# A hybrid decoder layer on one core: early weights loaded in 4 KB rows for two column groups in turn, and index queries computed for tokens 64 to 255 alone

## The chip, the cores and the metric

One core of a Trainium2 chip runs the kernel. The metric is device microseconds (us) of one execution, less is better. TensorE (PE) multiplies, VectorE (DVE), ScalarE (ACT) and GpSimd (POOL) prepare and collect, SyncE (SP) issues the loads, all from one queue in the order of the program. PEld is TensorE's load of the stationary operand.

## What is computed

256 tokens, width 4096, float32 in and out. The part that matters here:

```python
mod = jax.nn.silu(c) @ w_ada + b_ada               # 4096 x 12288
shift, scale, gate = jnp.split(mod, 3, axis=-1)
h = rms_norm(x, norm_g) * (1 + scale) + shift
z = h @ w_in                                       # 4096 x 15520
uA, vA, gA, qB, kB, vB, gB, qI, kI, wI = split(z)  # qI: 32 heads x 128 index queries
dots  = einsum('bqhd,bsd->bqhs', qI, kI)
score = einsum('bqh,bqhs->bqs', wI, relu(dots))    # causal; the best 64 keys of each query are kept
...                                                # attention, spatial gating, norms
x + gate * (concat([yA, yB]) @ w_out)
```

A query keeps min(256, 256/4) = 64 keys. Tokens 0 to 63 have at most 64 causal keys, so for them all causal keys are kept whatever the scores are.

## The kernel before

A float32 product is made of three fast ones. A weight tile `raw` is split into `whi` (ACT, L408: a rounded copy) and `wlo = raw - whi` (POOL and DVE, L414 and L416); h is kept as `hh` and `hl` in the same way. Then hh x whi, hl x whi and hh x wlo are summed in PSUM (`multiply`, L419).

The work is a list of steps, `stream`. One step takes 2 of the 32 chunks of 128 rows of a weight and up to 512 columns (one column group) and has 12 matmuls: 2 chunks x 3 products x 2 halves of 128 tokens. `step(t)` (L441) records, in this order, the load of the weights of step t + 3 (`load_w`, 4 buffers `raw`), the split of step t, the collecting of a group that ended two steps earlier (`add_to`, L793: PSUM is added to the group's sum in SBUF by two DVE additions), some of the side work, and the matmuls of step t.

The first 368 steps are the early stage, 8 blocks of 46 steps. A block has 4 chunks of h. It goes through 23 column groups of `w_in`: two of 336 columns (the last part of the index queries, the index key and the head weights, `kw`), and 21 of 512 (index queries `qi`, `v`, `u`, `q`, `k`, `vb`), 2 steps each. h of a block needs its columns of `w_ada`: while block b runs, the DVE op of L196 (called the ada op here) multiplies and adds 32 tiles `wa` for block b + 1, paced evenly by `pace` (L979), about 0.7 in a step. After each ada op the next `wa` is issued into its buffer (2 buffers). `pace(t)` stands before `step(t)`, so in SP's queue a `wa`, which waits for the ada op of that step, stands ahead of the `raw` of that step. On DVE the subtraction is given 320 of the 1024 columns of a step, POOL the other 704.

In block 7 no `wa` is left for h. There the indexer (L490) runs beside the steps: it turns the index queries of each head, multiplies them with the index keys, and adds up the scores. After the early stage come 8 gate groups of 16 steps and 8 output groups of 16 steps, with the attention beside them.

Of the kernel before, what the change touches and what calls it, by code (L numbers as in the profile page):

```python
# [15 lines left out]
P = 128  # L16
# [21 lines left out]
AHEAD = 3  # L38
# [4 lines left out]
def layer(ctx, tc, x, c, w_ada, b_ada, norm_g, w_in, ln_v_g, ln_v_b, w_s, b_s, q_norm_g,  # L43
# [213 lines left out]
    h_hi, h_lo = {}, {}  # L257
# [24 lines left out]

    def keep_h(b, hh, hl):
        for j in range(BLOCKS[b]):
            h_hi[starts[b] + j] = hh[:, j]
            h_lo[starts[b] + j] = hl[:, j]

    def first_h():
# [26 lines left out]
    def make_h(b, accs):  # L315
# [18 lines left out]
        for j in range(0, nk, 2):  # L334
            nc.gpsimd.tensor_sub(hl[:, j], hts[j // 2][:, 0], hh[:, j].bitcast(F32))
            nc.vector.tensor_sub(hl[:, j + 1], hts[j // 2][:, 1], hh[:, j + 1].bitcast(F32))
            if j + 2 == nk:
                keep_h(b, hh, hl)
# [38 lines left out]

    visits = []
    stream = []

    def visit(src, parts, ks, c0, w, read, soon=False, before=None):
        v = dict(src=src, parts=parts, ks=ks, c0=c0, w=w, read=read, soon=soon, before=before)
        visits.append(v)
        for i in range(0, len(ks), 2):
            stream.append((v, i))

    raws = {}
# [13 lines left out]
    def split(t):  # L401

        raw, w = raws.pop(t), stream[t][0]["w"]
        nk = raw.shape[1]
        hi = [sp.tile([P, 512], F32R, name="whi") for _ in range(nk)]
        lo = [sp.tile([P, 512], F32R, name="wlo") for _ in range(nk)]
        for kk in range(nk):
            nc.scalar.activation(hi[kk][:, :w], raw[:, kk, :w], AF.Copy)  # L408
        left = nk * pool_cols[0] * w // 1024 * 2
        for kk in range(nk):  # L410
            cut = w - min(left, w)
            left -= w - cut
            if cut:
                nc.vector.tensor_sub(lo[kk][:, :cut], raw[:, kk, :cut], hi[kk][:, :cut].bitcast(F32))  # L414
            if cut < w:
                nc.gpsimd.tensor_sub(lo[kk][:, cut:w], raw[:, kk, cut:w], hi[kk][:, cut:w].bitcast(F32))  # L416
        halves[t] = hi, lo

    def multiply(t):  # L419

        v, i = stream[t]
# [3 lines left out]
        (ah, al), w, n_k = v["parts"], v["w"], len(v["ks"])  # L425
        nk = len(hi)
        todo = [(part, kk, n) for kk in range(nk) for part in range(2) for n in range(NT)]
        todo += [(2, kk, n) for kk in range(nk) for n in range(NT)]
        if t + 1 == len(stream):
            todo.sort(key=lambda x: x[2])  # L430
        for part, kk, n in todo:
            k = v["ks"][i + kk]
            a = al if part == 1 else ah
            b = lo if part == 2 else hi
            nc.tensor.matmul(v["ps"][n][:, :w], a[k][:, n * P:(n + 1) * P], b[kk][:, :w],  # L435
                             start=(i + kk == 0 and part == 0),
                             stop=(i + kk == n_k - 1 and part == 2))
# [3 lines left out]
    def step(t):  # L441
        load_w(t + AHEAD)
# [10 lines left out]
        v, i = stream[t]  # L453
# [15 lines left out]
    groups["qi7"] = zp.tile([P, NT, 512], F32, name="qi7", tag="qi7")  # L469
    groups["kw"] = zp.tile([P, NT, 160], F32, name="kw", tag="kw")  # L470
    early.append((O_KW - 176, 336, [("qi7", 336, 176), ("kw", 0, 160)]))
    early.append((O_KW - 512, 336, [("qi7", 0, 336)]))
    for g in range(7):
# [16 lines left out]
    def indexer():  # L490
# [24 lines left out]
        wi = small([P, NT, IDX_HEADS], "wi")  # L515
        tp = misc()
# [11 lines left out]
        def turn(g, n):  # L528
            tp = misc()
            for hh in range(4):  # L530
# [546 lines left out]
```

## Time and profile before

| what | us |
|---|---|
| runs (3), median | 1887.4 (1884.28 to 1892.18) |
| the profiled execution's own time | 1888.63 |
| its span, first to last instruction | 1886.9 |
| PE busy | 1824.8 (97%) |
| DVE, POOL, ACT busy | 1447.4 (77%), 1295.3 (69%), 933.8 (49%) |
| bytes moved by DMA | 542.58 MB, 288 GB/s on the mean |

PE busy is the union of matmul records, whose ends are modelled, so it says that PE always had something, not that it ran at its best. A stage is judged by the start times of its matmuls.

### The profile page before, as it was taken

Reading aid. Unit: us, or ns where it says so; the run is one execution under the profiler, and the core shown is the slowest. Engines: PE = TensorE matmul, PEld = TensorE weight load, DVE = VectorE, ACT = ScalarE, POOL = GpSimd, SP = SyncE. Lnnn points to the kernel's source line nnn. Section 1 sums busy time; section 2 is a strip of 40 time slices with the busy share of each in tenths; the row PEclk is TensorE's granted clock in tenths of the full one; section 3 lists DMA queues with packets and bytes.
Section 4 is the critical chain, followed back from the end, with each engine's and each line's share of the span. In section 5 each row is a group of like instructions: output and inputs, shape, how many; then the busy total and the mean of one; then the engine's idle time right before and its main releaser. Section 6 shows DMA issues by size and latency. Waiting matters only on the chain. (4 is left out here: it accounts for less than half of the span.)

```text
span 1886.9 us, 27998 instructions
## 1 busy us (share of the span) xinstructions
PE 1824.8 (97%) x8324; PEld 1490.3 (79%) x8324; DVE 1447.4 (77%) x1762; ACT 933.8 (49%) x1737; POOL 1295.3 (69%) x1339
## 2 busy tenths in 40 slices
PE   5799999999999999999999999999999999999998
PEld 2487878878888888788888777787888888888887
DVE  4666888888888888888777898877777677677754
ACT  4356545344453454444445556566654554444443
POOL 0366777777777777777675546766567777877786
PEclk9899999999999999999999999999999999999999
DMA  9999998999989989999874477876789799899964
GB/s 311 339 338 340 332 322 304 331 316 306 335 304 322 321 300 324 328 309 340 284 207 146 128 224 262 272 257 202 242 281 312 248 323 338 295 307 350 334 212 156
DMA packets 269554, 542.58 MB, mean 288 GB/s; under 512 B 17270, under 2 KB 29784, under 8 KB 269404
## 3 DMA queue, kind: packets, MB, share of 16 engines
q1 hardware_dynamic: 269404, 540.79, 84.6%
q8 instruction: 68, 1.11, 0.2%
q14 instruction: 82, 0.67, 0.1%
HBM read 536.51 MB, written 4.22 MB: 287 GB/s over the span
## 5 line engine op out<-in xcount | busy, mean ns | idle before, releaser
L416 POOL TENSOR_TENSOR wlo<-raw,whi 128x512 fp32r<-128x512 f32 (+1 forms) x1248 | 1220.3, 1004 | 536.9 <-ACT whi L408 448.2
L408 ACT ACTIVATE whi<-raw 128x512 fp32r<-128x512 f32 (+1 forms) x1248 | 730.9, 619 | 834.9 <-DMA raw<-in_w_in_dram 407.5
L414 DVE TENSOR_TENSOR wlo<-raw,whi 128x320 fp32r<-128x320 f32 (+2 forms) x624 | 640.7, 1028 | 323.2 <-ACT whi L408 209.4
L435 PE MATMUL mm_ps<-whi,hh 128*128 128x512 f32 (+1 forms) x1984 | 620.4, 394 | 11.4 <-ACT whi L408 9.4
L435 PE MATMUL mm_ps<-whi,hl 128*128 128x512 f32 (+1 forms) x1984 | 604.9, 386 | 2.4 <-DVE hl L303 2.4
L435 PE MATMUL mm_ps<-wlo,hh 128*128 128x512 f32 (+1 forms) x1984 | 525.4, 386 | 5.7 <-DVE wlo L414 4.1
L196 DVE SCALAR_TENSOR_TENSOR acc<-wa,csil,acc 128x1024 f32<-128x1024 f32 x341 | 436.3, 1279 | 57.1 <-DMA wa<-in_w_ada_dram 56.4
L435 PEld LDWEIGHTS mm_ps<-wlo,hh 128*128 128x128 f32 x1984 | 368.9, 188 | 83.8 <-POOL wlo L416 8.8
L435 PEld LDWEIGHTS mm_ps<-whi,hh 128*128 128x128 f32 x1984 | 363.5, 189 | 90.2 <-ACT whi L408 19.9
L435 PEld LDWEIGHTS mm_ps<-whi,hl 128*128 128x128 f32 x1984 | 371.2, 188 | 77.3 <-DVE hl L303 2.9
L435 PE MATMUL mm_ps<-whi,yh 128*128 128x512 f32 x512 | 158.2, 390 | 0.0
L435 PE MATMUL mm_ps<-whi,yl 128*128 128x512 f32 x512 | 158.0, 389 | 0.0
L435 PE MATMUL mm_ps<-wlo,yh 128*128 128x512 f32 x512 | 137.5, 390 | 0.2
L435 PEld LDWEIGHTS mm_ps<-wlo,yh 128*128 128x128 f32 x512 | 95.9, 188 | 21.2 <-POOL wlo L416 1.5
L435 PEld LDWEIGHTS mm_ps<-whi,yh 128*128 128x128 f32 x512 | 95.9, 188 | 20.4 <-ACT whi L408 0.4
L435 PEld LDWEIGHTS mm_ps<-whi,yl 128*128 128x128 f32 x512 | 96.1, 188 | 20.0
L802 DVE TENSOR_TENSOR qi<-qi,mm_ps 128x512 f32<-128x512 f32 (+2 forms) x126 | 73.2, 616 | 0.0
L217 PE MATMUL acc<-wa,csil 128*1 128x512 f32 x64 | 28.1, 629 | 13.2 <-DMA wa<-in_w_ada_dram 13.2
L802 DVE TENSOR_TENSOR u<-u,mm_ps 128x512 f32<-128x512 f32 x56 | 35.6, 675 | 0.0
L802 DVE TENSOR_TENSOR v<-v,mm_ps 128x512 f32<-128x512 f32 x56 | 35.6, 675 | 0.0
L802 DVE TENSOR_TENSOR q<-q,mm_ps 128x512 f32<-128x512 f32 x56 | 35.6, 675 | 0.0
L222 DVE SCALAR_TENSOR_TENSOR accs<-wa,csil,accs 128x1024 f32<-128x1024 f32 x15 | 19.2, 1283 | 17.9 <-DMA wa<-in_w_ada_dram 17.8
(173 smaller groups left out, 797.2 us busy)
## 6 DMA issues: line engine op xcount, KB each, us to landing
raw<-in_w_in_dram SPq DMA_DIRECT2D x464, 512.0 KB, 5.9
wa<-in_w_ada_dram SPq DMA_DIRECT2D x384, 512.0 KB, 5.1
raw<-in_w_out_dram SPq DMA_DIRECT2D x128, 512.0 KB, 6.0
raw<-in_w_in_dram SPq DMA_DIRECT2D x32, 336.0 KB, 4.8
xs<-in_x_dram SPq DMA_DIRECT2D x8, 512.0 KB, 5.4
xres<-in_x_dram SPq DMA_DIRECT2D x8, 512.0 KB, 6.8
out_dram<-yt SPq DMA_DIRECT2D x16, 256.0 KB, 3.6
wk<-rb_d SPq DMA_DIRECT2D x16, 128.0 KB, 4.7
```

The costliest lines, as they stand in the source:

```text
L196: nc.vector.scalar_tensor_tensor(dst, src, csil[:, k:k + 1], dst, op0=OP.mult, op1=OP.add)
L217: nc.tensor.matmul(acc[g:g + 1, s, :w], csil[:, k:k + 1], wt[:, s], start=i < 4, stop=i >= KC // 2 - 4)
L222: nc.vector.scalar_tensor_tensor(accs, wt, csil[:, k:k + 1], accs, op0=OP.mult, op1=OP.add)
L408: nc.scalar.activation(hi[kk][:, :w], raw[:, kk, :w], AF.Copy)
L414: nc.vector.tensor_sub(lo[kk][:, :cut], raw[:, kk, :cut], hi[kk][:, :cut].bitcast(F32))
L416: nc.gpsimd.tensor_sub(lo[kk][:, cut:w], raw[:, kk, cut:w], hi[kk][:, cut:w].bitcast(F32))
L435: nc.tensor.matmul(v["ps"][n][:, :w], a[k][:, n * P:(n + 1) * P], b[kk][:, :w], start=(i + kk == 0 and part == 0), stop=(i + kk == n_k - 1 ...
L802: nc.vector.tensor_add(z, z, p)
```

## The change

Three things change together.

1. *Loads.* In the early stage `kw` becomes a group of its own, 160 columns, loaded as one tile of 4 chunks. The other 22 groups (8 `qi`, 14 others, all 512 wide) are taken in pairs. A load is one chunk and 1024 neighbouring columns (rows of 4 KB where they were 2 KB; 512 KB a load as before). A pair of groups goes: chunks 0 and 1 for its first group, the same chunks for its second, chunks 2 and 3 for the first, for the second. `load_w` now issues whatever fits into the 4 buffers; a buffer is free once both groups have been split.
2. *Index queries.* For the `qi` groups, `side_by_side` puts tokens 64 to 127 of h's two parts beside each other (`both`: 64 columns of hh, 64 of hl), so that one matmul with `whi` gives both products for them. The two rows of results are added in the indexer by a matmul with `fold` in place of the transposition. Tokens 0 to 63 are not computed, and their mask is set so that all their causal keys are kept.
3. *Order.* The additions of a group that ended come before the split of the step (`soon=b > 0`), and two `yield`s spread the side work of the later stages.

```diff
+    def side_by_side(b, hts):
+        both = s2.tile([P, BLOCKS[b], 2, 64], F32R, name="both", tag="s2")
+        for i, ht in enumerate(hts):
+            j = slice(2 * i, 2 * i + 2)
+            nc.scalar.activation(both[:, j, 0], ht[:, :, 64:P], AF.Copy)
+            nc.vector.tensor_sub(both[:, j, 1], ht[:, :, 64:P], both[:, j, 0].bitcast(F32))
+        for j in range(BLOCKS[b]):
+            h_both[starts[b] + j] = both[:, j].rearrange("p a b -> p (a b)")
...
+    def visit_pair(src, c0, v0, v1):
+        for i in range(0, len(v0["ks"]), 2):
+            m = [new_load(src, [k], c0, 1024) for k in v0["ks"][i:i + 2]]
+            stream.append((v0, i, [(m[0], 0), (m[1], 0)], 0))
+            stream.append((v1, i, [(m[0], 1), (m[1], 1)], 2))
...
-    def load_w(t):
-        if t >= len(stream) or t in raws:
-            return
-        v, i = stream[t]
-        nk, w, c0 = min(2, len(v["ks"]) - i), v["w"], v["c0"]
-        raw = wp.tile([P, 2, 512], F32, name="raw")
-        raw = raw[:, :nk]
-        nc.sync.dma_start(raw[:, :, :w], v["src"][:, v["ks"][i]:v["ks"][i] + nk, c0:c0 + w])
-        raws[t] = raw
+    def load_w():
+        while len(raws) < min(len(loads), split_loads[0] + WBUFS):
+            nk, w, src = loads[len(raws)]
+            raw = wp.tile([P, 1024], F32, name="raw")
+            raw = raw[:, :nk * w].rearrange("p (k w) -> p k w", k=nk)
+            nc.sync.dma_start(raw, src)
...
-        todo = [(part, kk, n) for kk in range(nk) for part in range(2) for n in range(NT)]
-        todo += [(2, kk, n) for kk in range(nk) for n in range(NT)]
+        for k, b in zip(ks, hi):
+            if v["packed"]:
+                todo += [(0, h_both[k], b), (1, half(ah, k, 1), b), (1, half(al, k, 1), b)]
+            else:
+                todo += [(n, half(a, k, n), b) for a in (ah, al) for n in range(NT)]
+        for k, b in zip(ks, lo):
+            todo += [(n, h_both[k] if v["packed"] and n == 0 else half(ah, k, n), b) for n in range(NT)]
...
     def step(t):
-        load_w(t + AHEAD)
+        load_w()
...
     for b, nk in enumerate(BLOCKS):
-        for c0, w, parts in early:
-            visit(w_in_t, (h_hi, h_lo), list(range(starts[b], starts[b] + nk)), c0, w, add_to(parts, b == 0),
-                  soon=0 < b and nk == 2)
+        ks = list(range(starts[b], starts[b] + nk))
+        vs = [new_visit((h_hi, h_lo), ks, w, add_to(parts, b == 0), packed=parts[0][0].startswith("qi"),
+                        soon=b > 0) for c0, w, parts in early]
+        visit(w_in_t, early[0][0], vs[0], per=nk)
+        for e in range(1, len(early), 2):
+            visit_pair(w_in_t, early[e][0], vs[e], vs[e + 1])
```

On SP, in the middle of block 0, the queue of before (a `wa` is a tile of `w_ada`, a `raw` one of `w_in`; what a row waits for stands in brackets):

```order
L178 DMA wa_1128<-in_w_ada_dram 128x2x512 [waits DMAHW6_49,DVE_49]
L396 DMA raw_1130<-in_w_in_dram 128x2x512 [waits DMAHW3_49,Pool_49]
L178 DMA wa_1156<-in_w_ada_dram 128x2x512 [waits DMAHW0_49,DVE_49]
L396 DMA raw_1158<-in_w_in_dram 128x2x512 [waits DMAHW5_49,Pool_49]
L178 DMA wa_1184<-in_w_ada_dram 128x2x512 [waits DMAHW2_49,DVE_49]
L396 DMA raw_1186<-in_w_in_dram 128x2x512 [waits DMAHW7_49,Pool_49]
```

And the same place in the changed kernel:

```order
L177 DMA wa_1181<-in_w_ada_dram 128x2x512 [waits DMAHW3_49,DVE_49]
L177 DMA wa_1209<-in_w_ada_dram 128x2x512 [waits DMAHW4_49,DVE_49]
L424 DMA raw_1211<-in_w_in_dram 128x1024 [waits DMAHW1_49,Pool_49]
L424 DMA raw_1213<-in_w_in_dram 128x1024 [waits DMAHW2_49,Pool_49]
L177 DMA wa_1237<-in_w_ada_dram 128x2x512 [waits DMAHW7_49,DVE_49]
L177 DMA wa_1261<-in_w_ada_dram 128x2x512 [waits DMAHW0_49,DVE_49]
L424 DMA raw_1263<-in_w_in_dram 128x1024 [waits DMAHW5_49,Pool_49]
L424 DMA raw_1265<-in_w_in_dram 128x1024 [waits DMAHW6_49,Pool_49]
```

Where one weight load was issued in each step, two are now issued in every second step, behind the `wa` of that step.

On DVE, in block 1 of the changed kernel, between the subtractions (`wlo`) of one pair of loads (`raw_3091`, first group, then second group) and the one after:

```order
L854 TENSOR_TENSOR qi0_167<-qi0_167,mm_ps_3051 128x512 [waits PE_49]
L854 TENSOR_TENSOR qi0_167<-qi0_167,mm_ps_3052 128x512 [waits PE_49]
L445 TENSOR_TENSOR wlo_3146<-raw_3091,whi_3144 128x320 [waits DMAHW4_49,Activation_49]
L195 SCALAR_TENSOR_TENSOR acc_2721<-wa_3113,csil_160,acc_2721 128x1024 [waits DMAHW5_49,DVE_49]
L854 TENSOR_TENSOR qi1_168<-qi1_168,mm_ps_3077 128x512 [waits PE_49]
L854 TENSOR_TENSOR qi1_168<-qi1_168,mm_ps_3078 128x512 [waits PE_49]
L445 TENSOR_TENSOR wlo_3172<-raw_3091,whi_3170 128x320 [waits Activation_49]
L445 TENSOR_TENSOR wlo_3197<-raw_3139,whi_3195 128x320 [waits DMAHW0_49,PE_49,Activation_49]
```

The two subtractions that free the buffer `raw_3091` now have an ada op and the two additions of the group before between them; in the kernel before one subtraction freed a buffer.

On PE, the first step of a `qi` group in the changed kernel (block 0):

```order
L476 MATMUL mm_ps_532<-whi_523,both_451 128x512
L476 MATMUL mm_ps_533<-whi_523,hh0_437 128x512
L476 MATMUL mm_ps_533<-whi_523,hl0_442 128x512
L476 MATMUL mm_ps_532<-whi_524,both_451 128x512
L476 MATMUL mm_ps_533<-whi_524,hh0_437 128x512
L476 MATMUL mm_ps_533<-whi_524,hl0_442 128x512
L476 MATMUL mm_ps_532<-wlo_525,both_451 128x512
L476 MATMUL mm_ps_533<-wlo_525,hh0_437 128x512
L476 MATMUL mm_ps_532<-wlo_526,both_451 128x512
L476 MATMUL mm_ps_533<-wlo_526,hh0_437 128x512
```

Such a step has 10 matmuls where it had 12.

## Rows read from the trace of the kernel before

**Rows 1.** Windows: block 0, blocks 1 to 6, block 7, all that follows.

```profile
core 0: us, PE busy (x) PEld busy (x) DVE busy (x) ACT busy (x) POOL busy (x), PEclk, DMA share, GB/s
70.30:202.60 132.30, 128.32 (x568) 106.17 (x569) 88.83 (x95) 79.05 (x150) 90.36 (x93) 0.96 0.94 328
202.60:961.40 758.80, 749.29 (x3409) 620.59 (x3409) 639.15 (x777) 342.81 (x609) 562.96 (x566) 1.00 0.92 315
961.40:1120.80 159.40, 156.53 (x768) 129.83 (x768) 132.80 (x194) 85.24 (x139) 90.42 (x94) 1.00 0.56 169
1120.80:1886.90 766.10, 751.22 (x3437) 619.66 (x3435) 553.97 (x652) 404.10 (x803) 546.87 (x576) 1.00 0.81 274
```

**Rows 2.** Timeline of PE: starts of two neighbouring steps, 512 wide, then 336 wide.

```profile
508.96 0.62 PE L435 MATMUL mm_ps<-whi,hh 128*128 128x512 f32 x2
...
511.68 0.39 PE L435 MATMUL mm_ps<-whi,hh 128*128 128x512 f32 x1
...
328.28 0.47 PE L435 MATMUL mm_ps<-whi,hh 128*128 128x336 f32 x2
...
330.12 0.47 PE L435 MATMUL mm_ps<-whi,hh 128*128 128x336 f32 x2
```

**Rows 3.** Timeline of PE: 16 matmuls with one column each.

```profile
67.17 1.95 PE L265 MATMUL ms_ps<-one,accs 128*128 128x1 f32 x16 [2.21 <-DVE accs L223]
```

**Rows 4.** Who waited for whom in blocks 1 to 6: total us, times, longest.

```profile
ACT whi L408 <- DMA raw<-in_w_in_dram: 305.2, 156, 4.4
...
ACT whi L408 <- PE mm_ps L435: 73.7, 59, 3.7
...
PEld mm_ps L435 <- ACT whi L408: 16.6, 23, 1.9
```

**Rows 5.** SP's own waits in blocks 1 to 6.

```profile
SPq L178 <- DVE acc L196: 272.8, 138, 3.9
```

**Rows 6.** Timeline of DVE in block 3: start, us, instruction, idle before.

```profile
503.40 1.28 DVE L196 SCALAR_TENSOR_TENSOR acc<-wa,csil,acc 128x1024 f32<-128x1024 f32 x1
504.95 1.16 DVE L414 TENSOR_TENSOR wlo<-raw,whi 128x320 fp32r<-128x320 f32 x1 [0.27 <-ACT whi L408]
506.04 1.27 DVE L802 TENSOR_TENSOR qi<-qi,mm_ps 128x512 f32<-128x512 f32 x2
507.23 1.28 DVE L196 SCALAR_TENSOR_TENSOR acc<-wa,csil,acc 128x1024 f32<-128x1024 f32 x1
508.42 0.81 DVE L414 TENSOR_TENSOR wlo<-raw,whi 128x320 fp32r<-128x320 f32 x1
...
511.17 0.49 DVE L414 TENSOR_TENSOR wlo<-raw,whi 128x320 fp32r<-128x320 f32 x1
```

**Rows 7.** Timeline of ACT and of SP there.

```profile
503.76 1.16 ACT L408 ACTIVATE whi<-raw 128x512 fp32r<-128x512 f32 x2 [1.49 <-PE mm_ps L435]
...
508.54 0.37 SPq L178 DMA_DIRECT2D wa<-in_w_ada_dram  x1
509.00 0.42 SPq L396 DMA_DIRECT2D raw<-in_w_in_dram  x1
```

**Rows 8.** DMA issues in blocks 1 to 6: count, KB, median us to landing.

```profile
raw<-in_w_in_dram SPq DMA_DIRECT2D x253, 512.0 KB, 6.2
```

**Rows 9.** DMA in block 7: GB/s in 40 slices, then the issues.

```profile
GB/s 228 227 227 238 211 191 154 216 162 136 136 127 137 150 182 103 213 141 132 132 151 143 208 32 134 130 132 0 145 253 60 275 192 265 58 391 353 129 192 68
...
raw<-in_w_in_dram SPq DMA_DIRECT2D x45, 512.0 KB, 4.1
wa<-in_w_ada_dram SPq DMA_DIRECT2D x3, 512.0 KB, 3.8
```

**Rows 10.** DMA issues after the early stage.

```profile
raw<-in_w_in_dram SPq DMA_DIRECT2D x124, 512.0 KB, 5.3
```

**Rows 11.** Groups of instructions like the new copies: ACT 128x128, DVE 128x256.

```profile
L620 ACT ACTIVATE junk<-q 128x128 f32<-128x128 f32 x32 | 9.4, 295 | 3.1 <-PE ms_ps L824 1.8 <-PE ms_ps L834 1.3
...
L336 DVE TENSOR_TENSOR hl<-ht,hh 128x256 fp32r<-128x256 f32 x12 | 7.5, 627 | 0.0
```

More of the change, by code (lines that the diff above doesn't have):

```diff
@@ L379, in layer, with new_visit, new_load, visit @@
     stream = []
[L381 to L387, printed above, removed]
-    def load_w(t):
-        if t >= len(stream) or t in raws:
-            return
-        v, i = stream[t]
-        nk, w, c0 = min(2, len(v["ks"]) - i), v["w"], v["c0"]
-        raw = wp.tile([P, 2, 512], F32, name="raw")
-        raw = raw[:, :nk]
-        nc.sync.dma_start(raw[:, :, :w], v["src"][:, v["ks"][i]:v["ks"][i] + nk, c0:c0 + w])
-        raws[t] = raw
+    loads = []
+    raws = []
+    split_loads = [0]
+    def new_visit(parts, ks, w, read, packed=False, soon=False, before=None):
+        visits.append(dict(parts=parts, ks=ks, w=w, read=read, packed=packed, soon=soon, before=before))
+        return visits[-1]
+    def new_load(src, ks, c0, w):
+        loads.append((len(ks), w, src[:, ks[0]:ks[0] + len(ks), c0:c0 + w]))
+        return len(loads) - 1
+    def visit(src, c0, v, per=2):
+        for i in range(0, len(v["ks"]), per):
+            m = new_load(src, v["ks"][i:i + per], c0, v["w"])
+            for j in range(0, per, 2):
+                stream.append((v, i + j, [(m, j), (m, j + 1)], int(j + 2 == per)))
+    def visit_pair(src, c0, v0, v1):
[9 more added lines that the diff above has]
+            nc.sync.dma_start(raw, src)
+            raws.append(raw.rearrange("p k (a w) -> p (k a) w", a=2) if w > 512 else raw)
     halves = {}
     def split(t):
-        raw, w = raws.pop(t), stream[t][0]["w"]
-        nk = raw.shape[1]
+        v, _, where, done = stream[t]
+        w = v["w"]
+        raw = [raws[m][:, j] for m, j in where]
+        nk = len(raw)
         hi = [sp.tile([P, 512], F32R, name="whi") for _ in range(nk)]
@@ L424, in multiply, with half @@
             v["ps"] = [mm.tile([P, 512], F32, name="mm_ps", tag="mm") for _ in range(NT)]
-        (ah, al), w, n_k = v["parts"], v["w"], len(v["ks"])
-        nk = len(hi)
-        todo = [(part, kk, n) for kk in range(nk) for part in range(2) for n in range(NT)]
-        todo += [(2, kk, n) for kk in range(nk) for n in range(NT)]
-        if t + 1 == len(stream):
[L430 to L437, printed above, removed]
+        (ah, al), w, ks = v["parts"], v["w"], v["ks"][i:i + len(hi)]
+        def half(a, k, n):
+            return a[k][:, n * P:(n + 1) * P]
+        todo = []
+        for k, b in zip(ks, hi):
[5 more added lines that the diff above has]
+            todo += [(n, h_both[k] if v["packed"] and n == 0 else half(ah, k, n), b) for n in range(NT)]
+        if t + 1 == len(stream):
+            todo.sort(key=lambda x: x[0])
+        ends = {n: max(j for j, x in enumerate(todo) if x[0] == n) for n in range(NT)}
+        begun = set() if i == 0 else {0, 1}
+        for j, (n, a, b) in enumerate(todo):
+            nc.tensor.matmul(v["ps"][n][:, :w], a, b[:, :w], start=n not in begun,
+                             stop=i + len(hi) == len(v["ks"]) and j == ends[n])
+            begun.add(n)
     reads = []
     def step(t):
-        load_w(t + AHEAD)
+        load_w()
         due = [v for u, v in reads if u <= t]
@@ L467, in add_group @@
         early.append((c0, w, [(name, 0, w)]))
[L469 to L473, printed above, removed]
+    add_group("kw", O_KW, 160)
+    for g in range(8):
         add_group(f"qi{g}", O_QI + 512 * g, 512)
@@ L967, in read @@
                     nc.sync.dma_start(out_t[:, n, 512 * g:512 * (g + 1)], t)
-            visit(w_out_t, (y_hi, y_lo), every, 512 * g, 512, read, before=before)
+            visit(w_out_t, 512 * g, new_visit((y_hi, y_lo), every, 512, read, before=before))
         for g in range(8):
@@ L1003, in begin_mixes @@
         nonlocal mixed
-        mixed = later(24, mixes(), 20)
+        mixed = later(28, mixes(), 21)
     def begin_gates():
@@ L1019, in layer @@
     first_h()
-    for t in range(AHEAD):
-        load_w(t)
+    load_w()
     load_ada()
```

64 lines of the change are left out of this document (41 added, 23 removed).

## The prediction

> **What bounds the kernel now.** I read the windows first, then the starts of the matmuls, then the waits, then the queues that the change touches. The windows [rows 1] cut the run into block 0 (132.3 us), blocks 1 to 6 (758.8 us, 126.5 each), block 7 (159.4 us) and the rest (766.1 us). The granted clock is 1.00, the 2.4 GHz level, in all of them but block 0 (0.96), so the clock explains nothing here. A full step takes 511.68 - 508.96 = 2.72 us for 12 matmuls, 0.227 us each; a step of 336 columns takes 330.12 - 328.28 = 1.84 us [rows 2]. A block of 4 x 1.84 + 42 x 2.72 is 121.6 us if PE never waits; the 16 small matmuls for h add 1.95 [rows 3]; the remaining 3.0 of the 126.5 us are stalls. So PE sets the pace of the early stage, but barely: the DMA engines are 92% busy [rows 1], ACT waited 156 times, 305.2 us, for weights to land, and 59 times for PE [rows 4], while PE's weight load waited only 16.6 us for ACT [rows 4]. The loads are late for ACT and just in time for PE. Block 7 is another matter: DMA share 0.56, PE busy 156.5 of 159.4 us [rows 1].
>
> Why the loads are just in time is seen as a loop: a buffer lands, is split, is freed, is loaded again, and serves four steps later. On DVE one subtraction takes 1.09 us when it had waited (504.95 to 506.04), two additions 1.19 us, an ada op 1.19 us (507.23 to 508.42) [rows 6]. In about 0.7 of the steps there is an ada op (32 in 46), 0.7 x 1.19 = 0.83 us; SP issues the weight load only after it, 0.46 us behind the `wa` [rows 7], and SP waited 272.8 us for just this op [rows 5]. Both copies on ACT take 1.16 us [rows 7], and a load 6.2 us to land [rows 8]: 1.16 + 1.09 + 1.19 + 0.83 + 6.2 = 10.5 us, against 4 x 2.72 = 10.88 us on PE.
>
> **The change, part by part.** *Matmuls.* Of a block's steps 28 stay at 2.72 us (76.2), 16 become packed with 10 matmuls (2.27 us each, 36.3), and two are `kw` with 160 columns. A matmul of one column takes 1.95 / 16 = 0.12 us [rows 3], one of 336 columns 0.15 [rows 2]; 160 columns lie between, nearer the first, so 24 take 3.0 us (3.7 at most). Sum 115.5 instead of 121.6: 6.1 us a block, 49 us in eight, if PE stays the bound.
>
> *Loads.* Now two buffers are issued together, every second step, behind the `wa` of that step, and a buffer is free only after two splits. The loop, again over four steps: second copy on ACT 0.58 (half of 1.16 [rows 7]); subtraction 1.09; ada op 0.83; the additions of the group before, which now stand ahead of the second subtraction, 1.19; second subtraction 0.81 [rows 6]; ada op 0.83. That is 5.33 us from landing to issue. The landing of a pair stands in no row. A lone load took 4.1 (`raw`) or 3.8 us (`wa`) in block 7, where the queue is short, and its best slice moved 391 GB/s, 1.34 us for 512 KB [rows 9]. With a `wa` ahead the second load lands after 3.8 + 2 x 1.34 = 6.5 us; without one (3 in 10) the first load leaves earlier and the second takes 4.1. The mean is 5.8, the loop 11.1 us. The bounds: with both subtractions at the 0.49 us of the quickest row [rows 6] and 5.7 us of landing the loop is 10.1; with the 6.2 us of blocks 1 to 6 [rows 8] and 1.34 for the second load it is 12.9. I take 11.1, since at most one `wa` is under way when a pair is issued, which is nearer to block 7 than to blocks 1 to 6, where up to three weight loads and two `wa` were under way. So the loop and not PE sets the pace: four packed steps, 9.07 us on PE, take 11.1, and four full ones stay at what they took before, (126.5 - 4 x 1.84 - 1.95) / 42 x 4 = 11.2.
>
> The trace shows 3.8 and 4.1 us for one load [rows 9]. The Trainium skill, "DMA: Bandwidth & Descriptors", section "Anatomy of one DMA", gives about 2.0 us fixed plus bytes over 436 GB/s, a fit for loads that GpSimd issues: 3.2 us for one, 5.6 us for the last of three, an estimate of 4.9 on the mean, and a loop of 10.2 us. SP issues these loads, and the rows have a duration, so I take the rows; by the page's fit the result would be the first rival below.
>
> *Longer rows.* No row separates 4 KB from 2 KB rows; the best slices of 2 KB rows already move 391 GB/s, above the 315 of blocks 1 to 6 [rows 1]. I count 0, and no loss.
>
> *Copies.* `both` is two ACT copies and two DVE subtractions of 128 columns a block. ACT's like row is 0.295 us, DVE's is 0.63 us for 256 columns [rows 11]; they stand between the steps of one pair: 0.7 us a block, between 0 (hidden) and 1.9 (all in the way). They also hold one of three scratch buffers while the indexer begins in block 7: 0 to 2 us, I take 1. Before the first matmul they cost 1 us.
>
> *Sum.* Blocks 1 to 6: 4 x 11.1 + 7 x 11.2 = 122.8, `kw` 3.5 (3.0, and 0.5 for the load behind it that now has only its short steps ahead), half of the 1.95, copies 0.7: 128.0, +1.5 each, +9. Block 0 collects on ACT, so the additions leave the loop: 5.33 - 1.19 + 0.45 for its denser ada ops (0.89 a step, 33 in 37), landing 6.2, 10.8 us; 4 x 10.8 + 7 x 11.2 + 5.2 and its 5.8 us of slow start are 132.6, 0. Block 7 has no ada ops and is PE's: -6.1 + 1 = -5. The start +1. After that the same work runs in the same order but for two pauses of side steps: 0, within 3 either way, since PE is busy 751 of 766 us [rows 1] with or without them. The sum is +5 us against the profiled execution's own 1888.6: 1894, and **1892 us** beside the median of the runs, which is 1.2 lower.
>
> **The rivals.** *The loads stay ahead (faster).* If the loop is under about 10.5 us, packed steps gain. For it: the low ends above; DVE's subtraction has been as short as 0.49 us [rows 6]. At 10.1 a block is 40.4 + 78.4 + 3.0 + 1.95 + 0.7 = 124.5 and the run 6 x -2.0, block 0 -2, block 7 -5, start +1: 1870. If no load is ever late, packed groups take 9.07 plus the old share of stalls, 9.3: 121.3 a block, 6 x -5.2 - 5 - 5 + 1: 1848. Against it: ACT already waits for weights in 156 of 276 steps [rows 4].
>
> *The pair loads queue up (slower).* At the 5.3 us of the later stages [rows 10], where the DMA share is 0.81 [rows 1], plus 1.34, landing is 6.6 and the loop 12.0: 11 x 12.0 + 4.2 = 136.2, +9.7 in each of six blocks, and +1 + 1 - 5 elsewhere: 1944. It decides from a loop of 11.5 us on. For it: a block loads as many bytes as before, in about the same time, which kept the DMA engines 0.92 busy. Against it: fewer loads are under way at once.
>
> *Nothing of it matters.* The new matmul order saves what the list of instructions says, 10 for 12, so that the change does not do what it says is excluded for PE; that longer rows slow each load by as much as packing saves is left at a few per cent.
>
> **How the numbers follow.** A measurement of this kernel can tell about 0.5%, 9.4 us, from no change: 1878 to 1897. The forecast (loop 10.6 to 11.5, 1876 to 1910) has 0.38, of which 0.08 fall below, 0.23 within, 0.07 above. The loads ahead: 0.33, all faster. The queue: 0.25, all slower. The last: 0.04, half within, half slower. Faster 0.41, same 0.25, slower 0.34. As both signs are likely, the range must take in both rivals: from 1842 (a little under the floor of 1848) to 1942, which leaves out the upper half of the second rival and the tail of the first, under 2 in 10.
>
> **What would show it.** Right: blocks 1 to 6 at 124 to 131 us, groups of four packed steps about as long as four full ones, PE waiting for ACT and ACT for weights far more than 16.6 us, block 7 at about 154 us. Wrong: packed groups at 9.1 to 9.5 us with blocks near 121 (first rival), or full groups over 11.5 us and blocks over 132 (second). A pair's second load landing in under 5 or over 7 us after the issue of its first would decide between them.

## The result, and the profile after

The changed kernel takes 2006.57 us (median of 6 runs, 1995.38 to 2011.25), the kernel before 1889.70 beside it (6 runs, 1884.28 to 1895.45). The ratio is 1.061, 95% interval 1.0576 to 1.0644: slower, and outside the range of the forecast. The profiled execution took 1995.38 us, its span is 1993.6; it is the shortest of the six, so its parts show 107 of the 117 us.

The windows of the changed kernel, cut at the same places as [rows 1] (block 0, blocks 1 to 6, block 7, all that follows), show where the time is.

```profile
core 0: us, PE busy (x) PEld busy (x) DVE busy (x) ACT busy (x) POOL busy (x), PEclk, DMA share, GB/s
67.90:212.20 144.30, 128.53 (x536) 100.50 (x537) 91.82 (x98) 79.47 (x150) 96.56 (x93) 0.96 0.86 297
212.20:1065.80 853.60, 771.72 (x3217) 578.78 (x3216) 584.08 (x776) 344.53 (x623) 565.70 (x565) 0.99 0.82 280
1065.80:1224.00 158.20, 154.98 (x766) 126.88 (x765) 120.43 (x193) 84.22 (x140) 87.96 (x94) 1.00 0.50 167
1224.00:1993.60 769.60, 754.98 (x3439) 622.10 (x3437) 558.65 (x653) 406.39 (x804) 550.69 (x577) 0.99 0.82 273
```

The span is 106.7 us longer than the 1886.9 before: the start -2.4, block 0 +12.0, blocks 1 to 6 +94.8 (142.3 each for 126.5), block 7 -1.2, the rest +3.5. Nearly all of it is lost in the seven blocks in which `wa` loads run. The same bytes moved, at a DMA share of 0.82 where it was 0.92, so the engines that transfer were not busier than before.

The lines have moved: in the changed kernel L439 is the copy on ACT, L445 and L447 the subtractions on DVE and POOL, L476 the matmuls, L195 the ada op, L854 the additions, L177 and L424 the issues of `wa` and `raw`. The waits of blocks 1 to 6, against [rows 4]:

```profile
ACT whi L439 <- DMA raw<-in_w_in_dram: 404.4, 193, 7.3
...
PEld mm_ps L476 <- ACT whi L439: 106.1, 116, 3.1
ACT whi L439 <- PE mm_ps L476: 76.3, 50, 5.4
PE mm_ps L476 <- ACT whi L439: 50.6, 64, 2.7
```

And SP's own wait there, against [rows 5]:

```profile
SPq L177 <- DVE acc L195: 473.9, 164, 6.3
```

ACT waits for weights in 193 cases instead of 156, with 7.3 us as the longest instead of 4.4, and now PE waits for ACT: 106.1 us at its weight load, where it was 16.6, and 50.6 at the matmul. In front of all that, SP stood 473.9 us (272.8 before) at the issue of a `wa`, waiting for an ada op.

The issues of blocks 1 to 6 say that a load itself, at its median, is hardly slower (6.2 before, [rows 8]):

```profile
raw<-in_w_in_dram SPq DMA_DIRECT2D x266, 512.0 KB, 6.4
wa<-in_w_ada_dram SPq DMA_DIRECT2D x182, 512.0 KB, 4.9
```

One turn of the loop, in the timeline (start, us, engine, line, instruction, and the idle time before it with what ended it), first of SP, with all that it issued:

```profile
555.75 3.17 SPq L177 DMA_DIRECT2D wa<-in_w_ada_dram  x2
559.01 0.89 SPq L424 DMA_DIRECT2D raw<-in_w_in_dram  x2
560.80 0.38 SPq L177 DMA_DIRECT2D wa<-in_w_ada_dram  x1
561.28 0.94 SPq L424 DMA_DIRECT2D raw<-in_w_in_dram  x2
567.72 3.17 SPq L177 DMA_DIRECT2D wa<-in_w_ada_dram  x2
570.98 0.89 SPq L424 DMA_DIRECT2D raw<-in_w_in_dram  x2
```

The same on ACT:

```profile
564.10 0.63 ACT L439 ACTIVATE whi<-raw 128x512 fp32r<-128x512 f32 x1 [4.26 <-DMA raw<-in_w_in_dram]
565.34 1.68 ACT L439 ACTIVATE whi<-raw 128x512 fp32r<-128x512 f32 x3 [0.60 <-DMA raw<-in_w_in_dram]
...
575.99 0.63 ACT L439 ACTIVATE whi<-raw 128x512 fp32r<-128x512 f32 x1 [4.47 <-DMA raw<-in_w_in_dram]
577.20 1.68 ACT L439 ACTIVATE whi<-raw 128x512 fp32r<-128x512 f32 x3 [0.57 <-PE mm_ps L476]
```

And on DVE:

```profile
566.00 0.49 DVE L445 TENSOR_TENSOR wlo<-raw,whi 128x320 fp32r<-128x320 f32 x1 [2.43 <-ACT whi L439]
566.41 1.28 DVE L195 SCALAR_TENSOR_TENSOR acc<-wa,csil,acc 128x1024 f32<-128x1024 f32 x1
567.60 1.28 DVE L854 TENSOR_TENSOR v<-v,mm_ps 128x512 f32<-128x512 f32 x2
568.80 0.48 DVE L445 TENSOR_TENSOR wlo<-raw,whi 128x320 fp32r<-128x320 f32 x1
569.20 1.28 DVE L195 SCALAR_TENSOR_TENSOR acc<-wa,csil,acc 128x1024 f32<-128x1024 f32 x1
```

Follow it from 565.34, when ACT takes the second load of a pair. DVE subtracts for the first group, does an ada op, the two additions, the subtraction for the second group (568.80 to 569.28): the two buffers are free, since GpSimd's share of that subtraction had ended at 568.76. But SP holds a `wa` that needs the next ada op (569.20 to 570.48), so the loads follow at 570.98: 5.64 us after 565.34. The second of them is taken at 577.20, after 6.22. (Its row names a matmul as what ended the wait; by the updates of its semaphore the load landed at 577.09.) Turn: 11.86 us for four steps.

The picture of SP is as telling. From 555.75 to 562.22 it issues three `wa` and four `raw`, seven loads of 512 KB; then, until 567.72, none. Loads come in bunches and queue behind each other.

Over the 108 pairs of blocks 1 to 6 that have such a predecessor in their block, the same reading gives on the mean: 4.82 us from the second load's first copy to the issue, 6.48 us from there until the first new load is taken, 7.73 until the second is: a loop of 12.55 us. The second load had landed 7.46 us after that issue, and in 81 of the 108 cases it was what the copy waited for. Four packed steps took 12.43 us and four full ones 12.77. In the kernel before, four steps of 512 columns took 11.3 us (the 14 groups that are not index queries).

### The profile page after: what moved, and what is told of

The parts are those of the page before. It is cut to its first block, busy times and chain, and to the rows that moved or that the text cites. A ratio compares the mean times of both kernels' runs of the same rounds, so it can differ in the third digit from the quotient of the medians.

```text
span 1993.6 us, 27629 instructions
## 1 busy us (share of the span) xinstructions
PE 1849.4 (93%) x8100; PEld 1442.5 (72%) x8100; DVE 1387.6 (70%) x1765; ACT 936.6 (47%) x1751; POOL 1304.4 (65%) x1340
## 5 line engine op out<-in xcount | busy, mean ns | idle before, releaser
L447 POOL TENSOR_TENSOR wlo<-raw,whi 128x512 fp32r<-128x512 f32 (+1 forms) x1248 | 1224.7, 1006 | 642.1 <-ACT whi L439 502.2
L439 ACT ACTIVATE whi<-raw 128x512 fp32r<-128x512 f32 (+1 forms) x1248 | 733.0, 619 | 938.2 <-DMA raw<-in_w_in_dram 507.8
L445 DVE TENSOR_TENSOR wlo<-raw,whi 128x320 fp32r<-128x320 f32 (+2 forms) x624 | 574.7, 922 | 504.7 <-ACT whi L439 374.1
L476 PE MATMUL mm_ps<-whi,hh 128*128 128x512 f32 (+1 forms) x1728 | 588.3, 405 | 48.1 <-ACT whi L439 19.4
L476 PE MATMUL mm_ps<-whi,hl 128*128 128x512 f32 (+1 forms) x1728 | 554.2, 390 | 1.5 <-DVE hl L312 1.5
L476 PE MATMUL mm_ps<-wlo,hh 128*128 128x512 f32 (+1 forms) x1728 | 493.7, 389 | 6.3 <-DVE wlo L445 4.2
L195 DVE SCALAR_TENSOR_TENSOR acc<-wa,csil,acc 128x1024 f32<-128x1024 f32 x341 | 436.5, 1280 | 27.4 <-DMA wa<-in_w_ada_dram 25.3
L476 PEld LDWEIGHTS mm_ps<-whi,hh 128*128 128x128 f32 x1728 | 316.2, 190 | 160.5 <-ACT whi L439 50.3
L476 PEld LDWEIGHTS mm_ps<-wlo,hh 128*128 128x128 f32 x1728 | 324.2, 190 | 77.4 <-POOL wlo L447 8.7
L476 PEld LDWEIGHTS mm_ps<-whi,hl 128*128 128x128 f32 x1728 | 325.5, 190 | 67.7 <-DVE hl L312 1.7
L476 PE MATMUL mm_ps<-whi,yh 128*128 128x512 f32 x512 | 158.3, 390 | 0.6 <-ACT whi L439 0.6
L476 PE MATMUL mm_ps<-whi,yl 128*128 128x512 f32 x512 | 158.0, 389 | 0.0
L476 PE MATMUL mm_ps<-whi,both 128*128 128x512 f32 x256 | 111.4, 435 | 47.9 <-ACT whi L439 32.9
L476 PE MATMUL mm_ps<-wlo,yh 128*128 128x512 f32 x512 | 137.6, 390 | 0.9 <-POOL wlo L447 0.9
L476 PEld LDWEIGHTS mm_ps<-whi,both 128*128 128x128 f32 x256 | 49.1, 192 | 89.3 <-ACT whi L439 61.0
L476 PEld LDWEIGHTS mm_ps<-wlo,yh 128*128 128x128 f32 x512 | 95.8, 188 | 22.2 <-POOL wlo L447 2.5
L476 PEld LDWEIGHTS mm_ps<-whi,yh 128*128 128x128 f32 x512 | 95.9, 188 | 21.1 <-ACT whi L439 1.2
L476 PEld LDWEIGHTS mm_ps<-whi,yl 128*128 128x128 f32 x512 | 96.1, 188 | 20.0
L476 PE MATMUL mm_ps<-wlo,both 128*128 128x512 f32 x256 | 101.9, 398 | 0.0
L854 DVE TENSOR_TENSOR qi<-qi,mm_ps 128x512 f32<-128x512 f32 x112 | 71.5, 678 | 5.4 <-PE mm_ps L476 5.3
L476 PEld LDWEIGHTS mm_ps<-wlo,both 128*128 128x128 f32 x256 | 49.4, 193 | 11.2
L854 DVE TENSOR_TENSOR v<-v,mm_ps 128x512 f32<-128x512 f32 x56 | 35.8, 681 | 8.1 <-PE mm_ps L476 8.1
## 6 DMA issues: line engine op xcount, KB each, us to landing
wk<-rb_d SPq DMA_DIRECT2D x16, 128.0 KB, 5.5
```

The lines of the kernel that those rows point to most:

```text
L195: nc.vector.scalar_tensor_tensor(dst, src, csil[:, k:k + 1], dst, op0=OP.mult, op1=OP.add)
L439: nc.scalar.activation(hi[kk][:, :w], raw[kk], AF.Copy)
L445: nc.vector.tensor_sub(lo[kk][:, :cut], raw[kk][:, :cut], hi[kk][:, :cut].bitcast(F32))
L447: nc.gpsimd.tensor_sub(lo[kk][:, cut:w], raw[kk][:, cut:w], hi[kk][:, cut:w].bitcast(F32))
L476: nc.tensor.matmul(v["ps"][n][:, :w], a, b[:, :w], start=n not in begun, stop=i + len(hi) == len(v["ks"]) and j == ends[n])
L854: nc.vector.tensor_add(z, z, p)
```

## Experiments

Times are medians; the ratio is to runs of the kernel before on the same chip, with its 95% interval. "Packed" and "full" are four steps, the mean over blocks 1 to 6. In "pairs alone" nothing is packed: 12.70 are its index-query steps with 12 matmuls. An edit is against the changed kernel where nothing else is said.

| kernel | us | ratio (interval) | block 0 | blocks 1 to 6, each | packed | full |
|---|---|---|---|---|---|---|
| before | 1889.7 | 1 | 132.3 | 126.5 | | 11.31 |
| changed | 2006.6 | 1.061 (1.0576-1.0644) | 144.4 | 142.3 | 12.43 | 12.77 |
| packing alone | 1894.6 | 1.0035 (1.0014-1.0055) | 132.7 | 127.9 | 10.82 | 11.46 |
| pairs alone | 1987.9 | 1.0527 (1.0509-1.0545) | 143.2 | 140.3 | 12.70 | 12.36 |
| pairs, 2 KB rows | 1977.0 | 1.0452 (1.0429-1.0475) | 150.7 | 138.7 | 11.83 | 12.61 |
| changed, weights ahead of `wa` | 1911.6 | 1.0122 (1.0104-1.0140) | 142.6 | 128.4 | 11.04 | 11.65 |
| changed, no early `wa` loads | 1832.5 | 0.9700 (0.9666-0.9733) | 123.0 | 118.3 | 9.14 | 11.30 |
| turns, one load a step | 1881.6 | 0.9963 (0.9949-0.9978) | 134.1 | 124.7 | 10.55 | 11.38 |
| turns, one load a step, weights ahead | 1887.5 | 0.9988 (0.9971-1.0006) | 132.8 | 126.4 | 10.85 | 11.44 |
| before, weights ahead | 1875.7 | 0.9916 (0.9897-0.9935) | 129.6 | 124.2 | | 11.14 |
| packing, weights ahead | **1866.6** | 0.9869 (0.9847-0.9892) | 134.6 | 122.4 | 10.28 | 11.24 |
| packing, weights ahead, early additions | 1882.4 | 0.9962 (0.9942-0.9983) | 131.4 | 126.2 | 11.22 | 11.24 |
| packing alone, ada op last | 1902.2 | 1.0065 (1.0040-1.0089) | 132.5 | 128.6 | 11.30 | 11.42 |
| packing, weights ahead, no early `wa` loads | 1822.8 | 0.9646 (0.9608-0.9685) | 122.1 | 117.0 | 9.08 | 11.14 |

**Which part costs: packing alone.** One load of 2 chunks x 512 columns a step, the groups one after the other, the additions after the split.

```diff
-        for e in range(1, len(early), 2):
-            visit_pair(w_in_t, early[e][0], vs[e], vs[e + 1])
+        for e in range(len(early)):
+            visit(w_in_t, early[e][0], vs[e], per=2)
```

> Packing alone: one group after the other, 2 KB rows, one load in each step, additions after the split, as in the kernel before; only the packed index queries and the own kw group are kept. If the loop of the pair loads is the cause (the loop theory), blocks 1 to 6 fall to 119 to 126 us each and the run to 1840 to 1880 us. If the packing, its copies or the smaller index queries cost the time (the packing theory), blocks stay at 138 us or more and the run over 1960 us. If 4 KB rows are themselves slow to land (the row theory), the run is also 1840 to 1880 us.

1894.57 us: neither a loss nor the gain expected. The packed steps need 9.07 us of PE in four and took 10.82. That the supply of weights holds them there is a reading at this point; the run below in which they fall to 9.08 once the `wa` loads are left out bears it out.

**Pairs alone.** No packing, index queries of all 256 tokens; `side_by_side` isn't called, and `fold` holds the first half of `flip` alone.

```diff
-        vs = [new_visit((h_hi, h_lo), ks, w, add_to(parts, b == 0), packed=parts[0][0].startswith("qi"),
+        vs = [new_visit((h_hi, h_lo), ks, w, add_to(parts, b == 0), packed=False,
```

> Pair loads alone: 4 KB rows and groups in turn as in the changed kernel, but all index queries as two plain halves with 12 matmuls a step and no copies. The loop theory: the loop of about 12.6 us for four steps is longer than PE's 10.9 with or without packing, so blocks 1 to 6 stay at 140 to 145 us and the run at 1995 to 2030 us, of which up to 10 for block 7. The packing theory: the run returns to about 1890 us. The row theory: as the loop theory.

1987.9 us: the pairs, with the turns and the early additions that come with them, carry nearly the whole loss. Next question: the rows of 4 KB, the issue of two loads at once, or the order behind the `wa`?

**Rows of 2 KB, everything else in pairs.** A load is again 2 chunks of one group, but two are issued together, and both buffers come free after the second split.

```diff
-            m = [new_load(src, [k], c0, 1024) for k in v0["ks"][i:i + 2]]
-            stream.append((v0, i, [(m[0], 0), (m[1], 0)], 0))
-            stream.append((v1, i, [(m[0], 1), (m[1], 1)], 2))
+            m = [new_load(src, v0["ks"][i:i + 2], c, 512) for c in (c0, c0 + 512)]
+            stream.append((v0, i, [(m[0], 0), (m[0], 1)], 0))
+            stream.append((v1, i, [(m[1], 0), (m[1], 1)], 2))
```

> The changed kernel with its loads issued in pairs as there, behind the ada op's load, but each load is two chunks of 512 columns in 2 KB rows and serves one step alone. This keeps the paired issue and takes away the row length and the sharing of a buffer by two steps. The loop theory: the first load serves the first step alone, so the loop begins at its landing, 1.3 us earlier than before: 12.6 becomes about 11.3 us, blocks 126 to 132 us, the run at 1900 to 1945 us. The row theory: 2 KB rows land as in the kernel before, the run returns to 1880 to 1895 us. If pairing alone costs everything: 1985 to 2010 us.

1976.95 us: most of the loss stays with 2 KB rows. That a step can begin as soon as its own load is there gave back 30 us at the median, less than expected, though block 0 grew from 144.4 to 150.7 us, which was not followed up. The issues of its blocks 1 to 6 land in the same time, 4 KB rows or not:

```profile
raw<-in_w_in_dram SPq DMA_DIRECT2D x266, 512.0 KB, 6.3
wa<-in_w_ada_dram SPq DMA_DIRECT2D x182, 512.0 KB, 4.9
```

**The order on SP.** The loads of weights are issued ahead of `pace(t)`, so ahead of the `wa` of the step; 4 KB rows and pairs stay.

```diff
+            load_w()
             if t < last:
                 pace(t)
...
     def step(t):
-        load_w()
```

> The changed kernel with one thing moved: a step's weight loads are issued before that step's ada op and its load, so that on SP they no longer stand behind that load. The loop theory: one ada op (0.8 us on the mean) and the transfer ahead (0.9 us on the mean) leave the loop of four steps, which falls from 12.6 to about 10.9 us; blocks 1 to 6 at 122 to 130 us, the run at 1880 to 1930 us. The row theory: landing of 4 KB rows stays as slow, so the run stays over 1970 us. The packing theory: over 1970 us.

1911.57 us: 95 of the 117 us are back by moving one call. Its window of blocks 1 to 6, SP's two largest waits there, and the issues:

```profile
214.00:984.50 770.50, 733.46 (x3218) 587.33 (x3218) 610.43 (x779) 357.62 (x620) 555.75 (x565) 0.99 0.90 310
```

```profile
SPq L177 <- DVE acc L195: 197.8, 156, 3.8
SPq L424 <- POOL wlo L447: 158.1, 159, 6.1
```

```profile
raw<-in_w_in_dram SPq DMA_DIRECT2D x264, 512.0 KB, 6.0
```

The wait for the ada op falls from 473.9 to 197.8 us, and weights now wait for what they should, the split that frees their buffer. Read pair by pair as above, the part from the copy to the issue falls from 4.82 to 3.77 us, the landing of the second load only from 7.73 to 7.44, the loop from 12.55 to 11.22. With 11 loops in a block that is 14.6 us; the blocks became 13.9 shorter. So the order acts on the chain from copy to issue and hardly on the landing. Block 0 keeps its loss (142.6): its loop went only from 12.52 to 12.29.

**The transfers of `wa` themselves.** Only two tiles of `w_ada` are loaded for blocks 1 to 7 and used again; all ada ops stay, and the results are other numbers. This takes away two things together: the transfers, and SP's waits to issue them.

```diff
+            if s0 == 0 and k0 != "norm":
+                early_ada.append(0)
+                if len(early_ada) > 2:
+                    ada_tiles.append(kept[len(early_ada) % 2])
+                    return
```

> The changed kernel, with only the first two tiles of w_ada for blocks 1 to 7 loaded and used 16 times each per block in place of 32 tiles (so shift and scale of those blocks are other numbers: the loads are left out, every ada op stays). Theory (the weight loads are late because they are issued behind the wa loads and share the queues with them): a pair then lands like lone loads, 4.1 and 5.4 us after the first issue, the chain of 4.8 us stays, so the loop is about 10.2 us; packed steps 10.2 us per four, full ones 11.2, blocks 1 to 6 about 124 us, the run 1875 to 1900 us. Rival (two loads issued together, into buffers that come free together, are late by themselves, with or without wa): the second load still lands 7 us or more after the first issue, blocks 1 to 6 at 136 us or more, the run above 1960 us.

1832.5 us, far below even the theory. The window of its blocks 1 to 6, and the issues:

```profile
192.20:902.00 709.80, 705.77 (x3217) 584.70 (x3216) 622.89 (x776) 370.25 (x620) 549.85 (x565) 1.00 0.61 200
```

```profile
raw<-in_w_in_dram SPq DMA_DIRECT2D x264, 512.0 KB, 3.8
```

PE is busy 705.77 of 709.80 us; blocks take 118.3 us where PE's floor by the prediction was 115.5 and 1.95 for the matmuls of h, and a load lands in 3.8 us, near the 4.1 and 3.8 of block 7 of the kernel before [rows 9]. Read pair by pair, the second load lands 5.28 us after the issue of the first, and its copy then waits for PE more often (71 of 108 cases) than for the load (15). So the rival here, that two loads issued together are late by themselves, is out. Pairs, 4 KB rows, turns and early additions together cost 10 us when no `wa` stands ahead of them or beside them: with one load a step, additions after the split and the same `wa` left out the run takes 1822.8 us.

> Packing alone with the weights ahead of wa, and the same wa loads left out for blocks 1 to 7. Theory (there the DMA engines, 0.94 busy in blocks 1 to 6, hold the packed steps at 10.3 us per four instead of PE's 9.07): without wa the loads stay ahead, packed steps 9.1 to 9.6, full ones 10.9 to 11.1, blocks 117 to 119 us, the run 1830 to 1848 us. Rival (the turn of the four buffers, through the splits on ACT, POOL and DVE, holds them): packed steps stay at 10.0 or more, blocks at 121 or more, the run 1860 to 1870 us.

This leaves the same loads out of the best kernel below: every block 117.0 us, packed steps 9.08, PE busy all of its window, and the run 7 us under the range of the theory. There too it is the `wa` loads that hold the packed steps at 10.28; with the same splits and buffers but no `wa`, the turn of the four buffers doesn't. Read load by load over the packed steps, the landing falls from 6.00 to 4.34 us, the part from the second copy to the issue only from 3.27 to 2.91: so most of the gain comes from fewer transfers beside the weights, and the smaller part from a shorter wait on SP. The windows of blocks 1 to 6, the best kernel first, then the same without `wa`:

```profile
204.30:938.80 734.50, 717.10 (x3218) 583.97 (x3217) 602.92 (x776) 361.60 (x620) 551.80 (x565) 1.00 0.94 325
```

```profile
191.40:893.10 701.70, 701.70 (x3217) 585.35 (x3216) 622.69 (x776) 372.15 (x620) 570.35 (x565) 1.00 0.69 203
```

With `wa` the DMA engines are 0.94 busy, 0.94 x 122.4 = 115 us a block, about as long as PE's 117. That is no measured floor of the transfers: 325 GB/s moved here, and the best slice of block 7 moved 391 [rows 9]. Whether both could be hidden wholly behind each other, no run shows.

**Turns without pairs.** Groups still alternate and their additions come early, but each step has its own load of 2 chunks x 512 columns, free after one split; then the same with the weights ahead.

```diff
-            m = [new_load(src, [k], c0, 1024) for k in v0["ks"][i:i + 2]]
-            stream.append((v0, i, [(m[0], 0), (m[1], 0)], 0))
-            stream.append((v1, i, [(m[0], 1), (m[1], 1)], 2))
+            for v, c in ((v0, c0), (v1, c0 + 512)):
+                m = new_load(src, v0["ks"][i:i + 2], c, 512)
+                stream.append((v, i, [(m, 0), (m, 1)], 1))
```

> The changed kernel with the groups still in turn and the additions still ahead of the split, but each load again two chunks of 512 columns in 2 KB rows, used and freed by one step. The loop theory: a buffer is freed by one subtraction and loads are issued one a step, so the loop is about 10.5 us as before; packing shows its gain, blocks 1 to 6 at 119 to 126 us, the run at 1840 to 1880 us, close to the run with packing alone. The row theory: the same. A rival that blames the turns or the early additions (PSUM is held by two groups at once): the run stays over 1950 us.

1881.58 us: without the common issue and release the loss is gone, with the `wa` still ahead. From the run with 2 KB rows in pairs, 1976.95 us, this kernel differs in nothing else: rows, turns, early additions, packing and the order on SP are the same. So the common issue and release are worth 95 us.

> The kernel with groups in turn and one 2 KB-row load a step, with each step's weight load issued ahead of that step's ada op and its load. If the supply loop is still what holds packing back (its four steps measured 10.55 us packed, against 9.07 on PE), taking the ada op and the transfer ahead out of it leaves about 9 us: blocks 1 to 6 at 117 to 121 us, the run at 1840 to 1862 us. If the DMA engines' bytes hold it (0.92 busy at 124 us a block), or DVE then waits for the w_ada tiles that now come second, the run stays within 10 us of 1881.6.

1887.52 us: a miss. Here the order that gave 95 us with pairs gave nothing.

**The order in the kernel before, and with packing alone.** The same move of one call, first in the kernel before, then with packing alone.

> The kernel before with one thing moved: a step's weight load is issued ahead of that step's ada op and its load. PE needs 123.6 us a block with no stall, 126.5 were measured. The loop theory: the 3 us of stalls shrink, 1870 to 1887 us. If w_ada tiles then come late for DVE instead: 1885 to 1905 us.

1875.67 us, within the range of the loop theory.

> Packing alone, with each step's weight load ahead of the ada op's. Packing alone took 10.82 us for four packed steps, no less than before; if the supply loop holds them there, this falls to 9.2 to 10 us, blocks to 119 to 123 us and the run to 1845 to 1870 us. If bytes or late w_ada tiles hold them, the run stays within 10 us of 1894.6.

1866.60 us, 1.3% faster than the kernel before: the best version of those that compute the layer, and it keeps what was right in the change, the packing. Its packed steps, 10.28, stay above the 9.2 to 10 that were expected. Packing, worth nothing behind the `wa`, now gives 9 us over the kernel before with the same order.

**Why the turns missed: the early additions.** The best kernel, with only the additions put ahead of the split.

```diff
-        vs = [new_visit((h_hi, h_lo), ks, w, add_to(parts, b == 0), packed=parts[0][0].startswith("qi"))
+        vs = [new_visit((h_hi, h_lo), ks, w, add_to(parts, b == 0), packed=parts[0][0].startswith("qi"),
+                        soon=b > 0)
```

> Packing alone with the weights first (1866.6 us), and now with the additions of a group that ended ahead of the split of the step, as the changed kernel has them. Theory (what stands on DVE ahead of the split that frees a buffer delays the next load, so the early additions are why groups in turn with the weights first, at 1887.5 us, gained nothing): packed steps 10.6 to 10.9 us per four, blocks 1 to 6 at 125 to 127.5 us, the run 1878 to 1890 us. Rival (taking the groups in turn is what cost there, and the place of the additions is free): blocks 121 to 123.5 us, the run 1860 to 1872 us.

1882.41 us: 16 us lost, packed steps 11.22 instead of 10.28, more than expected. In the packed steps the part from the second copy to the issue of the next load into that buffer grew from 3.27 to 3.86 us: what stands on DVE ahead of a split delays the load. This would account for most of what the turns with the weights ahead lose against the best kernel (21 us). Why turns with early additions are better than packing alone as long as the `wa` is ahead (1881.6 against 1894.6), no run settles.

**The ada op behind the step.** Packing alone, `pace(t)` recorded after `step(t)`.

```diff
-            if t < last:
-                pace(t)
-            elif t == last:
+            if t == last:
                 pool_cols[0] = POOL_REST
             step(t)
+            if t < last:
+                pace(t)
```

> Packing alone, with the paced ada op (and the wa load that it issues) recorded behind the whole step in place of ahead of it: SP has the weight load ahead of wa as with the weights first, and DVE splits before it does the ada op. Theory (the chain from landing to issue counts, and the ada op's 0.83 us is one of its terms): buffers come free some 0.8 us earlier than with the weights first alone, packed steps 9.5 to 10.0 us per four, blocks 118 to 121, the run 1848 to 1862 us. Rival (the DMA engines are what holds it): as with the weights first alone, blocks 121 to 123.5, the run 1862 to 1872 us; an ada op that comes later could also leave h late at the start of a block and cost a few us.

1902.2 us, and a flaw in my reasoning rather than in the theory. Within a step the weights stand ahead of the `wa`, but the queue goes on: the `wa` of step t stands ahead of the weights of step t + 1, and its ada op stands on DVE right behind the split of step t. That is the order of packing alone again, with the same wait on SP (275.7 us there in blocks 1 to 6, 305.7 here):

```profile
SPq L177 <- DVE acc L195: 305.7, 146, 3.9
```

With the weights ahead, the ada op that the next `wa` needs is done before the split that the next weights need; so the `wa` does not hold them up. That, and not which of the two comes first in a step, is what the move changes.

## Why the prediction was wrong

**The mechanism was right, and the landing was mis-sized.** The prediction said that the loop of the pair loads and not PE would set the pace, and that four full steps would take as long as four packed ones. Both hold: 12.77 and 12.43 us. The step that failed is the landing of a pair, put at 5.8 us because "at most one `wa` is under way when a pair is issued, which is nearer to block 7 than to blocks 1 to 6". It was 7.46 us on the mean until the second load had landed, and 7.73 until ACT took it. In the turn shown, two `wa` were issued in the 3.3 us ahead of a pair, and a third `wa` and a second pair followed within 3 us. By the issues and landings of the trace, two or more `wa` were under way at the issue of 64 of the 108 pairs, one at 41 and none at 3, and in 67 cases weight loads of an earlier pair were under way too. The numbers were in hand: 32 `wa` to 22 pairs in a block are 1.5 a pair, the queue printed with the change has two ahead of each pair, and by the prediction's own formula two ahead make 3.8 + 3 x 1.34 = 7.8 us. Nor does a pair without `wa` land in the 4.1 us that were taken for it: with no early `wa` at all the second load took 5.28, since the first is ahead of it. The lone loads of block 7 [rows 9] were the wrong neighbours; the right ones were the 6.2 us of [rows 8], and even with the 1.34 us for the second load behind it that was my upper end, 7.5.

Term by term:

- The chain from copy to issue: 5.33 predicted, 4.82 measured. The subtractions took 0.49 us each in the turn shown instead of 1.09 and 0.81, and part of that is taken back by the wait for a second ada op. This error hid a part of the other.
- The loop: 11.1 predicted, 12.55 measured; 11 x 1.45 = 16 us a block, against 142.3 - 128.0 = 14.3 found. With the measured loop in all 11 groups and the 4.2 us that the second rival has beside them, 11 x 12.55 + 4.2 = 142.3 us, the block as measured: the loop was the right price of a group, at the wrong size.
- Full groups: I kept them at 11.2 because they had taken that before; the loop holds for them too, 12.8. The forecast priced only four of the 11 groups of four steps by the loop, which hardly mattered at 11.1 and matters at 12.55.
- Block 0: 0 predicted, +12.0 found. Its loop was put at 10.8 and was 12.52: a chain of 5.26 for 4.59 and a landing of 7.27, until the second load was taken, for 6.2.
- Block 7: -5 predicted, -1.2 found. The matmuls saved are there, but I took the matmuls with `fold` as a one-for-one exchange. The groups of PE's instructions in block 7, before and then after, show 64 against 64 + 32:

```profile
L531 PE MATMUL ms_ps<-flip,qi 128*128 128x128 f32 x64 | 9.6, 272 | 0.0
```

```profile
L579 PE MATMUL ms_ps<-fold,qi 128*128 128x64 f32 x64 | 8.0, 268 | 0.0
L577 PE MATMUL ms_ps<-flip,qi 128*128 128x128 f32 x32 | 4.8, 271 | 0.0
```

  Packing saves 32 matmuls in a block, and the indexer adds 32 smaller ones. By the rows these groups are busy 12.8 us where it was 9.6, 3.2 us more, and -6.1 + 3.2 + 1 is -1.9; the 0.7 us left over were not followed up.
- The start (+1 predicted, -2.4) and the rest (0, within 3; +3.5): small, not followed up.
- Longer rows, counted 0: right, by the runs with 2 KB rows and without `wa`.

**The rivals.** "The pair loads queue up" was what happened, with the sign that was shown for it (full groups over 11.5, blocks over 132, a second load landing after 7 us). I priced its loop at 12.0, from the landing of the later stages, with block 0 at +1, and gave it 0.25. Its argument for itself, as many bytes through the same engines, fits the landing: taking the `wa` loads away brings it from 7.46 to 5.28 us, while the weights ahead of them, at a DMA share of 0.90, leave it at 7.12. It isn't the whole, since the order takes 1.05 us out of the chain, and the same bytes in single loads cost nothing. "The loads stay ahead" describes the kernel without early `wa` loads, at 1832.5 us even below its 1848. The time by the Trainium skill's fit ("DMA: Bandwidth & Descriptors", section "Anatomy of one DMA"), given there for a DMA that GpSimd issues, a landing estimated at 4.9 us, is further from the 7.73 measured than the value taken; for these loads, issued by SP and queued behind others, the trace disagrees with it.

What the prediction also had in hand and did not use is [rows 5]: SP's wait of 272.8 us for the ada op. I put 0.83 us for it into the chain, as one term of several. That isn't what made the forecast fail, since the chain came out shorter than forecast, but it is what could be taken out. The move of one call, which takes this wait out of the path of the weights, is worth 16 us in the kernel before (0.84%), 28 with packing alone and 95 in the changed kernel: with pairs, two loads and their two steps stand behind each such wait. (With turns and one load a step it gave nothing, 1887.5 against 1881.6.) How the 95 us of the common issue and release split between loads that land later because they are issued together and buffers that come free later isn't settled: more buffers or a second queue for `wa` were not tried.

## What to carry to other kernels

An in-order queue that issues loads is a chain of its own: for each load ask what stands ahead of it and what that waits for, and compare it with the instruction that frees the load's own buffer. Issuing and freeing two loads at a time from four buffers saved nothing in the landing and cost 95 us here, and a late issue became dearer (28 us with packing alone, 95 with pairs). To price a load's landing, count the other loads in the queue for each time that it is issued. A saving on the busiest engine counts only as far as the supply is ahead: test this by leaving the rival loads out, which here gave PE's own pace, 117 us a block, in one run. That removes the transfers and the waits to issue them together; to tell the two apart, time the landing and the part from copy to issue.

## What was not expected of the hardware

The granted clock, 1.00 in blocks 1 to 6 of the kernel before, fell to the lower level (0.50, 1.2 GHz) there in six stretches of 3.4 us, after steps in which PE had stood waiting for weights. Windows of the changed kernel before, in and after one of them:

```profile
226.00:236.00 10.00, 7.58 (x28) 4.64 (x26) 5.26 (x8) 2.56 (x6) 4.78 (x5) 1.00 0.90 298
237.20:240.60 3.40, 3.40 (x10) 2.63 (x9) 3.40 (x4) 1.11 (x3) 3.00 (x4) 0.50 0.45 140
241.00:251.00 10.00, 9.74 (x42) 7.46 (x41) 6.96 (x9) 3.45 (x7) 6.83 (x8) 1.00 0.88 301
```

PE was busy 7.58 of the 10 us ahead, and then ran 3.40 us at half the clock: at most 1.7 us lost, 10 in the six stretches. So late weights cost a little twice; over the runs of the changed kernel the mean clock was 0.974 to 0.989, and the run with the highest is the shortest. With no early `wa` loads the clock of blocks 1 to 6 is 1.00 again.
